# An encoder layer with a gated scan: gate activations spread over the filler, and three pieces of VectorE work handed to GpSimd's DMA and to ScalarE

## The chip, the cores and the metric

The kernel runs on one core of a Trainium2 chip. A core has five engines with queues of their own that run in order and wait for each other by semaphores: TensorE (PE, matmuls; PEld are its weight loads), VectorE (DVE), ScalarE (ACT), GpSimd (POOL) and SyncE (SP, which here only issues DMA transfers). The metric is the device time of one execution in microseconds (us); lower is better.

## The reference

One layer of an encoder over x of 1024 positions by 1024 channels, in float32:

```
h   = rmsnorm(x);  proj = h @ W_in          # 1024 x 8192: glu, q, v, z_f, z_b, og, gA, gB
A   = silu(layernorm(dwconv31(glu(..)))) @ pw
f_d = lb_d + (1 - lb_d) * sigmoid(z_d),  k_d = (1 - lb_d) * sigmoid(-z_d)    # d = forward, backward
S_t = diag(f_t) S_{t-1} + k_t v_t^T,     o_t = S_t^T q_t      # per head, once in each direction
B   = (headnorm(o_fwd + o_bwd) * silu(og)) @ W_o
x   = x + (sigmoid(gA) * A + sigmoid(gB) * B) @ W_out
x   = x + (silu(dwconv3(h2 @ W_gate)) * (h2 @ W_up)) @ W_down,  h2 = rmsnorm(x);  final rmsnorm
```

There are 8 heads of 128 by 128. f is clipped to [1e-6, 1]. What the change touches is the scan, the two lines with f_d and S_t.

## The kernel before, in words

Activations lie transposed: channels on the 128 partitions, positions along the free axis, in halves of 512. Every large matrix product is done as three matmuls of 128x128 by 128x512 (high times high, high times low, low times high, lines 143 to 145), because each operand is split into two parts: ScalarE rounds it (line 121) and VectorE or GpSimd subtracts (line 118). Most of the input projection and the feed-forward product go through a seven-product scheme (`pair_job`) whose weight sums are made by accumulating DMAs that GpSimd issues (line 238).

The stages follow each other: norm and GLU; projection, with the 31-tap convolution on VectorE beside it; then the scan over heads; then output projection and feed-forward.

**The scan.** A head of 1024 positions is two half heads of 512, 16 in all. The scan needs no sequential loop: products of the gates f are formed over blocks of 8 positions, and blocks are then joined pairwise at levels 8, 16, 32 and 64.

- `scan_inputs(i)` (line 741) loads q and the two z (forward, backward) of half head i on SP, and issues on ScalarE, for each direction, sigmoid(-z) into k (line 752), sigmoid(z) (line 753) and f (line 755); then VectorE clamps f (line 762). It is called two half heads ahead.
- `scan_base` (line 765) forms the products over 8 positions in the tile `DE`: a strided copy (line 780), multiplications (`tt`, line 730), a reciprocal (line 786), then `Qh`, `Kh`, `qF` and `kG`. It is stepped along one half head ahead.
- `scan_levels` (line 825) runs the four levels. At each, ScalarE copies kG into `A` (line 835), PE multiplies `A` with `qF` into a PSUM bank (line 838), VectorE multiplies kG and qF up for the next level, and the part of the product that belongs to the level goes into `S_t`: masked copies by VectorE at levels 8, 16 and 32 (lines 865, 869), two copies by ScalarE of 64 partitions at level 64 (line 873). The diagonal of the backward product is kept in `dg` (line 867; one buffer) and added to `S_t` at the end (line 885).
- `scan_states` transposes kG on PE, copies it as `kT` (ScalarE, line 896) and multiplies it with v (line 903); VectorE and ScalarE form the chunk states `Sf` and `Sb`.
- `outputs`, one head later, multiplies `S_t`, `Sf`, `Sb` with v and qF (line 944), squares (line 949, `jk`), takes the power by GpSimd (line 405), scales (line 963) and transposes.

**What sets the order.** PE's order is that of the source (manual schedule): between two steps of the scan, `between(fill)` puts 1.3 pieces of the remaining input projection, the filler `dense`, each of six matmuls, then two steps of the next half head's base, then one step of the previous head's outputs. There are seven such places in a half head. The other engines' orders are set by a planner that starts from the source's order and moves instructions by what it thinks is ready. Each tile has a fixed number of buffers (`zi` 3, `f`, `k` and `q` 2, `S` 3, `DE` and `dg` 1), and the writer of a buffer waits for its last reader.

```
            base = cur.result()
            ahead = Base(ins) if i + 1 < NI else None
            ins = scan_inputs(i + 2) if i + 2 < NI else None
```

Of the kernel before, what the change touches and what calls it, by code (L numbers as in the profile page):

```python
# [44 lines left out]
def tile_hybrid_encoder(  # L45
# [511 lines left out]
    m_32 = cp.tile([P, P], U8, name="m_32")  # L557

    def build_masks():
        it = mp.tile([P, P], I32, tag="tm", name=nm("it"), bufs=4)  # L560
        ip = mp.tile([P, P], I32, tag="tm", name=nm("ip"), bufs=4)
        G.iota(it, pattern=[[1, P]], base=0, channel_multiplier=0)
        G.iota(ip, pattern=[[0, P]], base=0, channel_multiplier=1)
        xo = mp.tile([P, P], I32, tag="tm", name=nm("xo"), bufs=4)
        V.tensor_tensor(xo, it, ip, op=ALU.bitwise_xor)
        fs = mp.tile([P, 4, P], F32, tag="tm", name=nm("fs"), bufs=4)
        V.tensor_copy(fs[:, 0, :], xo)
        V.tensor_tensor(fs[:, 1, :], it, ip, op=ALU.subtract)
        ge = fs[:, 1, :]
# [6 lines left out]
        for m, h in ((m_16, 16.0), (m_32, 32.0)):  # L576
            V.tensor_scalar(fs[:, 2, :], fs[:, 0, :], h, None, op0=ALU.is_ge)
            V.tensor_scalar(fs[:, 3, :], fs[:, 0, :], 2 * h, None, op0=ALU.is_lt)
            V.tensor_tensor(m, fs[:, 2, :], fs[:, 3, :], op=ALU.mult)

    build_masks()

# [155 lines left out]
    def c4(t):  # L738
        return t.rearrange("p (c t) -> p c t", c=4)

    def scan_inputs(i):


        h, half = divmod(i, 2)
        q = page(hp, "q", 2)
        f = hp.tile([P, 2, H], F32, tag="f", name=nm("f"), bufs=2)
        kk = hp.tile([P, 2, H], F32, tag="k", name=nm("k"), bufs=2)
        nc.sync.dma_start(q, d_q[h][half])
        for d in range(2):
            z = page(hp, "zi", 3)  # L750
            nc.sync.dma_start(z, d_z[d][h][half])
            A.activation(kk[:, d, :], z, AF.Sigmoid, scale=-1.0)
            A.activation(z, z, AF.Sigmoid)
            fo = view(f, d * H + 7 * d, [[8, NB], [1 - 2 * d, 8]])
            A.activation(
                fo,
                z.rearrange("p (b e) -> p b e", e=8),
                AF.Identity,
                scale=oml_of(d, h),
                bias=lb_of(d, h),  # L760
            )
        V.tensor_scalar(f, f, MIN_FORGET, 1.0, op0=ALU.max, op1=ALU.min)
        return q, f, kk, kscale[:, h : h + NH + 1 : NH]

    def scan_base(ins):


        q, f, kk, ks = ins
# [11 lines left out]
        V.tensor_copy(ed(2, D + 4), fv(3, 4))  # L780
# [24 lines left out]
        along = [[8, NB], [1, 8]]  # L805
        for d in range(2):
            m0, st = ((0, 1), (7, -1))[d]
            whole = [[8, NB], [st, 8]]
            tt(view(Qh, (1 - d) * H + m0, whole), view(q, m0, whole), view(DE, D + d * H, along))
            yield  # L810
            keys(
                view(Kh, d * H + m0, whole),
                view(kk, d * H + m0, whole),
                ks[:, d : d + 1],
                view(DE, d * H, along),
            )
            yield
        both = [[H, 2], [8, NB], [1, 8]]
        tt(view(qF, 0, both), view(Qh, 0, both), view(fm, 0, [[NB, 2], [1, NB], [0, 8]]))
        yield  # L820
        tt(view(kG, 0, both), view(Kh, 0, both), view(DE, D + 7, [[H, 2], [8, NB], [0, 8]]))
        yield
        yield qF, kG, [(Qh[:, 1 - d, :], Kh[:, d, :]) for d in range(2)], tb

    def scan_levels(base, S_t, Tt):
# [31 lines left out]
        for h in (8, 16, 32, 64):  # L857
# [3 lines left out]
            if h == 8:  # L861
                A.copy(S_t, b)
                for d, m in ((0, m_f), (1, m_b)):
                    bi = inside(d)
                    V.copy_predicated(S_t, over(m), bi)
                    if d == 1:
                        V.copy_predicated(c4(dg), over(m_d), bi)
            elif h < 64:
                V.copy_predicated(S_t, over(m_16 if h == 16 else m_32), b)
            else:  # L870
                for s0 in range(0, P, h):
                    t0 = s0 ^ h
                    A.copy(S_t[s0 : s0 + h, :, t0 : t0 + h], b[s0 : s0 + h, :, t0 : t0 + h])
# [11 lines left out]
        V.tensor_tensor(S_t, S_t, c4(dg), op=ALU.add)  # L885

    def scan_states(i, kG, v, Tt, Sf, Sb):

# [122 lines left out]
            bm[h][half] = split(hx(), hx(), load(d_bm[h][half]), V)  # L1011

    NI = 2 * NH
    cur = Base(scan_inputs(0))
    ins = scan_inputs(1)
    dense.fill(21)
    pending = Stream(iter(()))
    for h in range(NH):
# [4 lines left out]
        for half in range(2):  # L1023
            i = 2 * h + half
            base = cur.result()
            ahead = Base(ins) if i + 1 < NI else None
            ins = scan_inputs(i + 2) if i + 2 < NI else None
# [355 lines left out]
```

## Time and profile before

| | |
|---|---|
| median of 3 runs | 1885.06 us (1883.33 to 1894.11) |
| the profiled execution | 1885.96 us |
| its span in the profile | 1884.2 us |
| PE, DVE, ACT, POOL busy | 95%, 67%, 42%, 11% of the span |
| the scan in the trace | about 560 to 957 us |

The profile is of one execution. A row of a group gives line, engine, operation, what it writes from what, shape and count, then busy time in all, mean ns of one, and the idle time of the engine just before, with what ended it. A row of the waits gives who waited for whom, us in all, times, and the longest. A row of a table of stretches gives, for each engine, busy us and instructions in the stretch, then the granted clock of TensorE, the share of the DMA engines and GB/s. A row of the timeline gives start, length, engine, line and operation; in brackets stands idle time before it and what ended it.

### The profile page before, as it was taken

What the parts mean: (1) busy time and instruction counts of PE and PEld (TensorE: products, weight loads), DVE (VectorE), ACT (ScalarE), POOL (GpSimd) and SP (SyncE); (2) the same over time, 40 slices, a digit from 0 to 9 for tenths busy, and PEclk for the clock granted to TensorE, in tenths of its full rate; (3) what the DMA queues carried; (4) which work ended last, traced back from release to release, by engine and by line L of the source; (5) the groups of instructions that cost most, each with busy time, mean ns of one, the idle gap of its engine ahead of it and who ended that gap; (6) DMA issues with size and microseconds to landing.
All of it is one profiled execution on the core that took longest, in us unless ns stands there. A gap on an engine that the chain in (4) does not pass through costs nothing.

```text
span 1884.2 us, 23705 instructions
## 1 busy us (share of the span) xinstructions
PE 1790.5 (95%) x8543; PEld 1478.6 (78%) x8543; DVE 1270.1 (67%) x1860; ACT 797.2 (42%) x1488; POOL 198.0 (11%) x202
## 2 busy tenths in 40 slices
PE   6988999999999999999989999899999999999996
PEld 4767877877787888888878778688888788788885
DVE  3488999635459999989935556676666767534445
ACT  6333343324554655555442144543443434522124
POOL 3101112213100000000000000111111111000000
PEclk9999999999999999999999999999999999999998
DMA  7747788876572333322228666777676766633134
GB/s 264 222 116 165 181 183 204 188 177 156 176 224 79 118 96 117 109 91 93 84 90 240 194 193 185 165 164 145 145 160 147 154 140 129 216 97 94 55 92 162
DMA packets 322764, 282.99 MB, mean 150 GB/s; under 512 B 14798, under 2 KB 244950, under 8 KB 322646
## 3 DMA queue, kind: packets, MB, share of 16 engines
q1 hardware_dynamic: 270854, 240.57, 41.2%
q0 software_dynamic: 51792, 40.90, 15.6%
q8 instruction: 67, 1.10, 0.2%
q14 instruction: 51, 0.42, 0.1%
HBM read 189.14 MB, written 71.83 MB: 139 GB/s over the span
## 4 chain that ended last, share of the span: by engine, by line
PE 48%; DVE 21%; DMA 18%; ACT 6%; issue 4%; POOL 2%; SPq 0%; ACTq 0%; DVEq 0%; POOLq 0%
PE mm L143 12%; PE mm L144 12%; PE mm L145 12%; DMA wr<-wr 3%; DMA tm<-d_a 3%; DVE wp L118 2%; DMA wr<-sw 2%; PE sc L143 2%; PE sc L145 2%; PE sc L144 2%; DVE kG L730 2%; DMA sw<-in_w_in_dram 2%; DVE acc L645 2%; DMA wr<-in_w_in_dram 2%; DVE qF L730 2%
## 5 line engine op out<-in xcount | busy, mean ns | idle before, releaser
L143 PE MATMUL mm<-hx,wp 128*128 128x512 f32 x1176 | 481.4, 409 | 19.4 <-ACT su L266 5.1
L145 PE MATMUL mm<-hx,wp 128*128 128x512 f32 x1176 | 467.2, 397 | 4.3 <-DVE wp L118 4.3
L144 PE MATMUL mm<-hx,wp 128*128 128x512 f32 x1176 | 466.1, 396 | 2.4 <-POOL hx L118 2.4
L121 ACT CAST wp<-wr 128x1024 fp32r<-128x1024 f32 (+2 forms) x196 | 179.7, 917 | 341.8 <-PE mm L144 207.9
L118 DVE TENSOR_TENSOR wp<-wr,wp 128x1024 fp32r<-128x1024 f32 (+2 forms) x196 | 207.2, 1057 | 118.7 <-ACT wp L121 113.0
L143 PEld LDWEIGHTS mm<-hx,wp 128*128 128x128 f32 x1176 | 225.7, 192 | 69.5 <-ACT su L266 7.2
L145 PEld LDWEIGHTS mm<-hx,wp 128*128 128x128 f32 x1176 | 224.8, 191 | 55.6 <-DVE wp L118 6.7
L144 PEld LDWEIGHTS mm<-hx,wp 128*128 128x128 f32 x1176 | 225.6, 192 | 47.9 <-POOL hx L118 4.7
L645 DVE SCALAR_TENSOR_TENSOR acc<-gl,v_b,acc 128x1024 f32<-128x1024 f32 x120 | 149.3, 1279 | 0.5
L1259 DVE TENSOR_TENSOR xr<-mm,xr 128x512 f32<-128x512 f32 x48 | 33.2, 691 | 80.9 <-PE mm L145 80.9
L238 POOL DMA_DIRECT2D wr<-sw x39 | 34.6, 888 | 491.1 <-DVE wp L118 227.6
L838 PE MATMUL sc<-qF,A 128*128 128x128 f32 x512 | 68.8, 277 | 13.8 <-DVE qF L730 13.2
L838 PEld LDWEIGHTS sc<-qF,A 128*128 128x128 f32 x512 | 64.3, 192 | 21.1 <-issue 17.0
L121 ACT CAST wq<-sw 128x1024 fp32r<-128x1024 f32 x39 | 41.0, 1052 | 78.2 <-PE mm L144 68.5
L835 ACT COPY A<-kG 128x512 f32<-128x512 f32 x64 | 39.6, 618 | 73.3 <-DVE kG L730 50.8
L143 PE MATMUL mm<-hy,wp 128*128 128x512 f32 x156 | 62.3, 399 | 6.7 <-ACT wp L121 5.2
L1181 DVE SCALAR_TENSOR_TENSOR tm<-gp,v_a,tm 128x512 f32<-128x512 f32 x88 | 65.7, 748 | 2.3 <-ACT tm L1177 1.1
L266 ACT COPY su<-mm 128x512 f32<-128x512 f32 x78 | 45.3, 581 | 49.9 <-PE mm L145 49.7
L144 PE MATMUL mm<-hy,wp 128*128 128x512 f32 x156 | 62.1, 398 | 0.0
L145 PE MATMUL mm<-hy,wp 128*128 128x512 f32 x156 | 61.7, 396 | 0.0
L143 PE MATMUL sc<-hy,wq 128*128 128x512 f32 x156 | 61.3, 393 | 0.0
L143 PE MATMUL tr<-hx,wp 128*128 128x512 f32 x156 | 61.3, 393 | 0.0
(289 smaller groups left out, 3587.7 us busy)
## 6 DMA issues: line engine op xcount, KB each, us to landing
wr<-in_w_in_dram SPq DMA_DIRECT2D x55, 512.0 KB, 5.3
sw<-in_ffn_w_up_dram SPq DMA_DIRECT2D x44, 256.0 KB, 3.6
sw<-in_ffn_w_up_dram POOLq DMA_DIRECT2D x22, 512.0 KB, 8.9
wr<-in_ffn_w_up_dram SPq DMA_DIRECT2D x22, 512.0 KB, 5.2
d_g<-ft SPq DMA_DIRECT2D x44, 256.0 KB, 5.6
ev<-d_g SPq DMA_DIRECT2D x44, 256.0 KB, 2.8
wr<-sw POOLq DMA_DIRECT2D x39, 256.0 KB, 3.3
wr<-wr POOLq DMA_DIRECT2D x39, 256.0 KB, 4.4
```

The source lines that it names most:

```text
L118: eng.tensor_tensor(lo, src, hi.bitcast(F32), op=ALU.subtract)
L121: A.copy(hi, src)
L143: T.matmul(acc, whi[:, k, :], ahi, start=first, stop=False, skip_group_check=again)
L144: T.matmul(acc, whi[:, k, :], alo, start=False, stop=False, skip_group_check=again)
L145: T.matmul(acc, wlo[:, k, :], ahi, start=False, stop=last, skip_group_check=again)
L238: G.dma_start(o, a, accum_op=ALU.add)
L266: A.copy(t, acc)
L645: V.scalar_tensor_tensor(acc, g[:, k : k + S], tap(k), acc, op0=ALU.mult, op1=ALU.add)
L730: V.tensor_tensor(o, a, b, op=op)
L835: A.copy(A_t.rearrange("p (b x e) -> p b x e", x=2, e=h), pairs(kG, h))
L838: T.matmul(b[:, c * P : (c + 1) * P].rearrange("p (b x e) -> p b x e", x=2, e=h), A_t[:, c * P : (c + 1) * P], view(qF, c * P, [[2 * h, P ...
L1181: V.scalar_tensor_tensor(c, g[:, o + k : o + k + H], vec("fdw", k * NF + j), c, op0=ALU.mult, op1=ALU.add,)
```

## The change

Four edits in the scan, none elsewhere but for one mask that is no longer built:

1. `scan_inputs` becomes a class `Inputs`. Its three loads are issued at once; its six gate activations come one at a time, one at each of the `between` places, and whatever is left when the base begins. The clamp of f moves to the beginning of `scan_base`.
2. The strided copy into `DE` is done by ScalarE (`A.copy`) in place of VectorE.
3. Level 32 goes into `S_t` by four ScalarE copies of 32 partitions, as level 64 does with two of 64, in place of a masked copy by VectorE; `m_32` is gone.
4. `dg` is added to `S_t` by an accumulating DMA that GpSimd issues, in place of an addition by VectorE.

```diff
-    def scan_inputs(i):
-        h, half = divmod(i, 2)
-        q = page(hp, "q", 2)
-        f = hp.tile([P, 2, H], F32, tag="f", name=nm("f"), bufs=2)
-        kk = hp.tile([P, 2, H], F32, tag="k", name=nm("k"), bufs=2)
-        nc.sync.dma_start(q, d_q[h][half])
-        for d in range(2):
-            z = page(hp, "zi", 3)
-            nc.sync.dma_start(z, d_z[d][h][half])
-            A.activation(kk[:, d, :], z, AF.Sigmoid, scale=-1.0)
-            A.activation(z, z, AF.Sigmoid)
...
+    class Inputs:
+        def __init__(self, i):
+            h, half = divmod(i, 2)
+            q = page(hp, "q", 2)
+            f = hp.tile([P, 2, H], F32, tag="f", name=nm("f"), bufs=2)
+            kk = hp.tile([P, 2, H], F32, tag="k", name=nm("k"), bufs=2)
+            zs = [page(hp, "zi", 3) for _ in range(2)]
+            nc.sync.dma_start(q, d_q[h][half])
+            for d, z in enumerate(zs):
+                nc.sync.dma_start(z, d_z[d][h][half])
+            self.parts = (q, f, kk, kscale[:, h : h + NH + 1 : NH])
+            self.todo = self.make(h, f, kk, zs)
+
+        def make(self, h, f, kk, zs):
+            for d, z in enumerate(zs):
+                A.activation(kk[:, d, :], z, AF.Sigmoid, scale=-1.0)
+                yield
+                A.activation(z, z, AF.Sigmoid)
+                yield
+                fo = view(f, d * H + 7 * d, [[8, NB], [1 - 2 * d, 8]])
+                A.activation(fo, z.rearrange("p (b e) -> p b e", e=8), AF.Identity,
+                    scale=oml_of(d, h), bias=lb_of(d, h))
+                yield
+
+        def step(self):
+            next(self.todo, None)
+
+        def result(self):
+            for _ in self.todo:
+                pass
+            return self.parts
+
+    def scan_base(ins):
+        q, f, kk, ks = ins.result()
         V.tensor_scalar(f, f, MIN_FORGET, 1.0, op0=ALU.max, op1=ALU.min)
-        return q, f, kk, kscale[:, h : h + NH + 1 : NH]
...
-        V.tensor_copy(ed(2, D + 4), fv(3, 4))
+        A.copy(ed(2, D + 4), fv(3, 4))
...
-            elif h < 64:
-                V.copy_predicated(S_t, over(m_16 if h == 16 else m_32), b)
+            elif h == 16:
+                V.copy_predicated(S_t, over(m_16), b)
             else:
                 for s0 in range(0, P, h):
                     t0 = s0 ^ h
                     A.copy(S_t[s0 : s0 + h, :, t0 : t0 + h], b[s0 : s0 + h, :, t0 : t0 + h])
...
-        V.tensor_tensor(S_t, S_t, c4(dg), op=ALU.add)
+        G.dma_start(S_t.rearrange("p c t -> p (c t)"), dg, accum_op=ALU.add)
...
                 pending.fill(1)
+                if ins is not None:
+                    ins.step()
```

More of the change, by code (lines that the diff above doesn't have):

```diff
@@ L556, in tile_hybrid_encoder @@
     m_16 = cp.tile([P, P], U8, name="m_16")
-    m_32 = cp.tile([P, P], U8, name="m_32")
     def build_masks():
@@ L575, in build_masks @@
         V.tensor_tensor(m_b, fs[:, 2, :], fs[:, 3, :], op=ALU.mult)
[L576 to L579, printed above, removed]
+        V.tensor_scalar(fs[:, 2, :], fs[:, 0, :], 16.0, None, op0=ALU.is_ge)
+        V.tensor_scalar(fs[:, 3, :], fs[:, 0, :], 32.0, None, op0=ALU.is_lt)
+        V.tensor_tensor(m_16, fs[:, 2, :], fs[:, 3, :], op=ALU.mult)
     build_masks()
@@ L739, in c4 @@
         return t.rearrange("p (c t) -> p c t", c=4)
-    def scan_inputs(i):
-        h, half = divmod(i, 2)
-        q = page(hp, "q", 2)
-        f = hp.tile([P, 2, H], F32, tag="f", name=nm("f"), bufs=2)
-        kk = hp.tile([P, 2, H], F32, tag="k", name=nm("k"), bufs=2)
-        nc.sync.dma_start(q, d_q[h][half])
-        for d in range(2):
-            z = page(hp, "zi", 3)
-            nc.sync.dma_start(z, d_z[d][h][half])
[L752 to L761, printed above, removed]
+    class Inputs:
[17 more added lines that the diff above has]
+                fo = view(f, d * H + 7 * d, [[8, NB], [1 - 2 * d, 8]])
+                A.activation(
+                    fo,
+                    z.rearrange("p (b e) -> p b e", e=8),
+                    AF.Identity,
+                    scale=oml_of(d, h),
+                    bias=lb_of(d, h),
+                )
+                yield
[5 more added lines that the diff above has]
+            return self.parts
@@ L762, in scan_inputs @@
+    def scan_base(ins):
+        q, f, kk, ks = ins.result()
         V.tensor_scalar(f, f, MIN_FORGET, 1.0, op0=ALU.max, op1=ALU.min)
-        return q, f, kk, kscale[:, h : h + NH + 1 : NH]
-    def scan_base(ins):
-        q, f, kk, ks = ins
         def two(t, *r):
@@ L1013, in tile_hybrid_encoder @@
     NI = 2 * NH
-    cur = Base(scan_inputs(0))
-    ins = scan_inputs(1)
+    cur = Base(Inputs(0))
+    ins = Inputs(1)
     dense.fill(21)
@@ L1026, in tile_hybrid_encoder @@
             ahead = Base(ins) if i + 1 < NI else None
-            ins = scan_inputs(i + 2) if i + 2 < NI else None
+            ins = Inputs(i + 2) if i + 2 < NI else None
             def between(fill):
```

## The prediction

> **What bounds the kernel now.** I read the page first: its head gives the span, its part 1 the busy share of each engine.
>
> ```profile
> span 1884.2 us, 23705 instructions
> PE 1790.5 (95%) x8543; PEld 1478.6 (78%) x8543; DVE 1270.1 (67%) x1860; ACT 797.2 (42%) x1488; POOL 198.0 (11%) x202
> ```
>
> TensorE is busy in 95% of the span, so over the whole kernel nothing but its idle time, some 94 us, can be won without taking matmuls away, and the change takes none. But the change touches one stage alone, the scan over heads, so the second view is the table of stretches, cut where the first and the last matmul of the scan's levels (L838) stand: a stretch ahead of it, the scan, a stretch behind it.
>
> ```profile
> core 0: us, PE busy (x) PEld busy (x) DVE busy (x) ACT busy (x) POOL busy (x), PEclk, DMA share, GB/s
> 530.00:560.00 30.00, 30.00 (x134) 24.75 (x133) 18.94 (x28) 18.77 (x30) 1.07 (x3) 1.00 0.72 227
> 560.00:957.00 397.00, 375.79 (x2403) 330.99 (x2402) 366.39 (x679) 214.88 (x493) 13.73 (x14) 1.00 0.33 101
> 957.00:1000.00 43.00, 38.85 (x200) 32.38 (x199) 15.47 (x26) 19.56 (x49) 1.83 (x2) 0.96 0.39 126
> ```
>
> In the scan two engines are nearly full: PE 375.79 of 397.00, DVE 366.39 of 397.00. ACT has 182 us free and POOL nearly everything. PE's idle time is 397.00 - 375.79 = 21.2 us over 16 half heads; that is the ceiling of any gain here, 1.1% of the kernel. What ends it is in the view of waits, asked for PE in this stretch.
>
> ```profile
> engine line waited for: us in total, times, longest us
> PE sc L838 <- DVE qF L730: 13.2, 11, 2.8
> PE sc L903 <- ACT kT L896: 5.4, 6, 1.3
> PE sc L851 <- ACT Sb L921: 1.8, 2, 1.5
> PE sc L838 <- ACT A L835: 0.5, 1, 0.5
> ```
>
> So two links are late, by about a microsecond at a time: DVE, which must update qF before the next level's matmuls (13.2 us), and ScalarE, which must copy kT before the states' matmuls (5.4 us). The change works on both: it takes load off the first and puts load on the second.
>
> **Part by part.** The groups of DVE in the scan, by line and shape:
>
> ```profile
> L869 DVE COPY_PREDICATED S<-m,sc 128x512 f32<-128x512 uint8 x32 | 23.4, 732 | 0.1
> L885 DVE TENSOR_TENSOR S<-S,dg 128x512 f32<-128x512 f32 x16 | 10.7, 669 | 0.3
> L762 DVE TENSOR_SCALAR f<-f 128x1024 f32<-128x1024 f32 x14 | 9.5, 680 | 4.4 <-ACT f L755 4.4
> L780 DVE COPY DE<-f 128x256 f32<-128x256 f32 x14 | 6.1, 434 | 0.0
> ```
>
> Removed from DVE per half head: one of the two L869 (level 32), L885, L780. Their durations sum to 732 + 669 + 434 = 1835 ns, but neighbours overlap, so what the queue gets back is the distance from one start to the next:
>
> ```profile
> 698.99 0.72 DVE L869 COPY_PREDICATED S<-m,sc 128x512 f32<-128x512 uint8 x1
> 699.60 0.68 DVE L730 TENSOR_TENSOR qF<-qF,tb 128x512 f32<-128x512 f32 x1
> ...
> 702.37 0.70 DVE L885 TENSOR_TENSOR S<-S,dg 128x512 f32<-128x512 f32 x1
> 702.98 1.22 DVE L730 TENSOR_TENSOR qF<-Qh,fm 128x1024 f32<-128x1024 f32 x1
> ```
>
> 0.61 for L869, 0.61 for L885; the same 0.1 off L780 gives about 0.33 (an estimate). That is 1.55 us per half head, 25 us over 16, so DVE goes from 366 to about 341 us busy. L869 stands directly ahead of the qF update that PE waits for. A wait of PE on qF averages 13.2 / 11 = 1.2 us, less than the 1.55 us given back in each half. The longest, 2.8 us, is more than that. I take 10 of the 13.2 us as gone: bounds 0 (if another instruction of that chain is then late) and 13.2.
>
> Added to ScalarE per half head: four copies of 32 partitions by 128 elements from PSUM (level 32), one strided SBUF copy of 256. No row has 32 partitions; the nearest are these.
>
> ```profile
> L835 ACT COPY A<-kG 128x512 f32<-128x512 f32 x64 | 39.6, 618 | 73.3 <-DVE kG L730 50.8 <-PE sc L838 12.7 <-DVE tb L730 9.9
> L873 ACT COPY S<-sc 64x256 f32<-64x256 f32 x32 | 11.6, 363 | 15.6 <-PE sc L838 15.3
> L923 ACT COPY Sb<-sc 128x128 f32<-128x128 f32 x8 | 2.2, 273 | 0.0
> ```
>
> From 128 elements to 256 the cost goes 273 to 363 ns whatever the partitions, so four copies are 4 x 0.27 = 1.1 us; for the strided one I take 0.4 us (between 0.36 and 0.62). So ScalarE gets 1.5 us more per half, 24 us in all: 215 to 239 of under 397. As load that is nothing; what counts is what stands behind it in the queue. Level 32's copies can start once its matmuls end, where DVE's copy did; their bank is not needed before the states' matmuls, behind level 64.
>
> **The moved gates.** In the old order six gate activations stood in one block behind Kh; then came the squares (jk), GpSimd's power (L405) on their sums, four scalings, and only then the second kT copy that PE waits for. One half head of the first kind in each head:
>
> ```profile
> 674.58 1.15 ACT L752 ACTIVATE k<-zi 128x512 f32<-128x512 f32 x2 [1.51 <-DVE Kh L733]
> 675.64 1.14 ACT L753 ACTIVATE zi<-zi 128x512 f32<-128x512 f32 x2
> 677.14 0.82 ACT L755 ACTIVATE f<-zi,lbw 128x512 f32<-128x512 f32 x1
> 678.84 0.37 ACT L873 COPY S<-sc 64x256 f32<-64x256 f32 x1
> 680.35 0.19 ACT L949 ACTIVATION_READ_ACCUMULATOR jk<-tm 128x1 f32 x1
> 682.60 1.28 ACT L963 ACTIVATE tm<-tm,ors 128x128 f32<-128x128 f32 x4 [1.35 <-POOL ors L405]
> 683.78 0.56 ACT L896 COPY kT<-tr 128x512 f32<-128x512 f32 x1
> ```
>
> (The columns are start, length and instruction; `x2` are two in a row.) In the changed program's order the strided copy takes the head of this block and waits for the same Kh; so the old wait is kept, not removed. Of the gates one sigmoid goes behind the squares (-0.5 us), but one or two copies of A for the next half head (0.6 us each in L835) now stand ahead of the last square, with the strided copy (0.4), and in some heads an evacuation stands ahead of the second kT. Against Kh the second kT comes, by these durations, between 0.2 and 2.4 us later than its old 683.78 - 674.58 = 9.2 us. Kh itself comes up to 1.55 us earlier per half given back on DVE. These two cancel within about a microsecond either way, so I take 0 of the 7.2 us of waits on kT and Sb as gone: bounds -7.2 (all gone) and +2.4 x 8 = +19 (no cover from DVE).
>
> The strided copy is also a new wait for DVE, ahead of its second product into DE: behind Kh stands qF, 1.22 us, then kG, against 0.4 us for the copy, so it is ready in time. On SP the loads of q and both z are now issued together, in their old order, ahead of the gates; the first gate waits for Kh today and not for its load:
>
> ```profile
> L752 ACT ACTIVATE k<-zi 128x512 f32<-128x512 f32 x26 | 15.2, 624 | 15.5 <-DVE Kh L733 15.4
> ```
>
> A load that is held up by its buffer for as long as the gates are spread stays hidden, since the buffer's last reader runs in the half head before. I take 0.
>
> The clamp (L762) is later in the source, but DVE's order is the planner's: in the changed program it stands just behind the reciprocal of the head before, a few instructions later than it did. It costs the same 680 ns; its 4.4 us of waiting may come or go with the last gate. DVE has about 2.9 us per half free after the change (397 - 341 over 16, less PE's own gain) to hide that. I take 0. Behind it in DVE's queue stand the Sf updates, which PE reads in the next head.
>
> **The accumulating DMA.** Its like exists already, issued by GpSimd at the same 256 KB, SBUF to SBUF:
>
> ```profile
> L238 POOL DMA_DIRECT2D wr<-sw x39 | 34.6, 888 | 491.1 <-DVE wp L118 227.6
> wr<-sw POOLq DMA_DIRECT2D x39, 256.0 KB, 3.3
> wr<-wr POOLq DMA_DIRECT2D x39, 256.0 KB, 4.4
> ```
>
> 0.9 us of GpSimd and 3.3 to 4.4 us to land. It adds two waits: the matmuls on S (L944), and the next write of dg (one buffer), with the kG update behind it in DVE's queue.
>
> ```profile
> 701.59 0.74 ACT L873 COPY S<-sc 64x256 f32<-64x256 f32 x2 [3.09 <-PE sc L838]
> ...
> 715.14 0.73 DVE L867 COPY_PREDICATED dg<-m_d,ob 128x512 f32<-128x512 uint8 x1
> 718.72 0.38 PE L944 MATMUL ob<-v,S 128*128 128x128 f32 x2
> ```
>
> S is complete at 702.33; 0.9 + 4.4 makes 707.6, 7.5 us ahead of the write at 715.14 and 11 ahead of the first matmul on any S. It stays hidden. In GpSimd's queue the power stands behind this issue, but in the half head shown above S is complete at 679.21 and the last square's sum at 680.54, 1.3 us later, which covers 0.9. Cost 0. Without that cover the power would be late by at most 0.9 us in 8 halves, 7 us. DMA engines are 0.33 busy here and PE waits on no weights.
>
> [...]
>
> ```profile
> L645 DVE SCALAR_TENSOR_TENSOR acc<-gl,v_b,acc x120: 1267/1280/1286, 118.8 to 349.4; 128x1024 f32<-128x1024 f32 x120
> L118 DVE TENSOR_TENSOR wq<-w,wq x39: 683/691/2421, 89.8 to 1592.1; 128x512 fp32r<-128x512 f32 x39
> 461.57 2.42 DVE L118 TENSOR_TENSOR wq<-w,wq 128x512 fp32r<-128x512 f32 x1
> 461.83 3.31 POOL L659 TENSOR_TENSOR tm<-tm,cx 128x512 f32<-128x512 f32 x2
> ```
>
> L645 has two SBUF inputs and runs where GpSimd issues such DMAs all along, yet its slowest is 6 ns above its median: issuing costs DVE nothing. The outlier of 2421 ns stands beside GpSimd's arithmetic (L659). [...]
>
> The three mask instructions removed cost under 1 us once, in a stretch where PE is full: 0.
>
> **Sum.** The profiled execution took 1885.96 us, 1.8 outside its span; the median of the runs is 1885.06, so one stands for the other. 1886 - 10 = **1876 us**, 0.5% faster.
>
> **Rivals.**
> *PE's idle time vanishes.* With DVE 25 us lighter and the gates no block any more, all four rows of waits go: 1886 - 21 = 1865. For it: PE would be the bound by far. Against it: the kT chain still passes through GpSimd's power.
> *ScalarE becomes the late link.* The second kT comes 2.4 us later in every first half of a head: 8 x 2.4 = 19 us, less the 10 of qF: 1895, slower. It decides from where the delay exceeds the 1.55 us that Kh gains. For it: the row with 1.35 us of waiting on POOL; against it: only some heads have the worse order.
> *The change does not do what it says*: the planner puts gates and clamp back, and DVE's free time is only idle, because qF waits on PE's own round trip. 1885.
> *Issuing blocks DVE after all*: 16 x 0.89 = 14 us of the 25 come back, and of the 10 about 4 stay: 1882.
>
> **Chances.** Forecast (1868 to 1882) 0.55; PE's idle time gone (1862 to 1868) 0.15; ScalarE late (1888 to 1905) 0.14; nothing 0.11; blocked issues 0.05. The range leaves out the upper half of the slow case and a little at the bottom: 1864 to 1892. A measurement of this kernel can tell about 1% from no change: below 1866 faster, above 1904 slower. Half of the second case lies below 1866 (0.08); of the slow case a quarter above 1904 (0.04); within, 0.88.
>
> **What would show it.** Right: in the scan DVE is near 341 us and ACT near 239 us busy, the row of PE waiting for qF falls from 13.2 to about 3 us, no DVE wait on the DMA at the dg write, and L903's wait on kT stays near 5 us. Wrong: L903's row grows beyond 15 us, or L838's stays above 10, or a wait of DVE on ScalarE's strided copy appears.

## The result, and the profile after

The changed kernel takes 1886.33 us (median of 20 runs) where the kernel before takes 1882.92 us (20 runs beside them). The ratio of the runs side by side is 1.0022, with a 95% interval of 1.0011 to 1.0032 (that of the two medians is 1.0018). It is 0.2% slower; forecast were 0.5% less. The busy shares on the changed kernel's page:

```profile
PE 1791.3 (95%) x8543; PEld 1481.3 (79%) x8543; DVE 1246.0 (66%) x1809; ACT 823.3 (44%) x1568; POOL 212.5 (11%) x218
```

VectorE lost 24 us and ScalarE took 26. The same stretch as in the prediction, and TensorE's waits in it (columns as there; in the changed file L853 is the levels' matmul, L728 the products, L911 the kT copy, L918 the states' matmul):

```profile
560.00:957.00 397.00, 375.08 (x2392) 331.49 (x2391) 346.83 (x632) 238.93 (x570) 27.85 (x29) 0.99 0.38 110
```

```profile
PE sc L918 <- ACT kT L911: 9.7, 6, 3.0
PE sc L853 <- DVE qF L728: 8.6, 6, 2.8
PE ob L918 <- ACT kT L911: 2.8, 3, 1.7
```

TensorE is idle for 397.00 - 375.08 = 21.9 us, against 21.2 before. The waits on qF fell by 4.6 us, from 13.2 to 8.6, and those on kT rose by 7.1, from 5.4 to 9.7 + 2.8 = 12.5 (two rows: the matmul on the second kT copy of a half head and that on the first). With the smaller rows the listed waits are 20.9 us before and 21.9 after: what came off the one link went to the other.

The parts themselves, by groups of ScalarE's instructions and the list of DMA issues:

```profile
L888 ACT COPY S<-sc 32x128 f32<-32x128 f32 x64 | 16.4, 256 | 17.0 <-PE sc L853 16.2
L795 ACT COPY DE<-f 128x256 f32<-128x256 f32 x16 | 11.2, 700 | 15.1 <-DVE Kh L731 15.0
```

```profile
S<-dg POOLq DMA_DIRECT2D x16, 256.0 KB, 3.5
```

A copy of 32x128 takes 256 ns (the 128x128 row of the prediction had 273), the strided copy 700 ns (and ScalarE waits 15 us in all in front of it), and the accumulating DMA lands 3.5 us after its issue.

**Where kT became late.** One half head of the kernel before and the one that answers to it after, each from the timeline (the squares, the transposes, the scalings that wait for GpSimd's power, the second kT copy; before also the first gate behind Kh and the matmul on kT):

```profile
723.64 0.31 ACT L949 ACTIVATE jk<-tm 128x128 f32<-128x128 f32 x1
...
724.21 1.15 ACT L752 ACTIVATE k<-zi 128x512 f32<-128x512 f32 x2 [0.17 <-DVE Kh L733]
...
730.49 0.30 ACT L949 ACTIVATE jk<-tm 128x128 f32<-128x128 f32 x1
...
731.85 0.60 PE L894 MATMUL tr<-ident,kG 128*128 128x128 f32 x4
...
733.59 1.28 ACT L963 ACTIVATE tm<-tm,ors 128x128 f32<-128x128 f32 x4 [1.29 <-POOL ors L405]
734.78 0.56 ACT L896 COPY kT<-tr 128x512 f32<-128x512 f32 x1
...
735.40 1.16 PE L903 MATMUL sc<-v,kT 128*128 128x128 f32 x8 [0.66 <-ACT kT L896]
```

```profile
723.34 0.68 ACT L795 COPY DE<-f 128x256 f32<-128x256 f32 x1 [1.85 <-DVE Kh L731]
723.92 0.31 ACT L964 ACTIVATE jk<-tm 128x128 f32<-128x128 f32 x1
...
731.40 0.60 PE L909 MATMUL tr<-ident,kG 128*128 128x128 f32 x4
...
733.45 0.31 ACT L964 ACTIVATE jk<-tm 128x128 f32<-128x128 f32 x1
...
735.92 1.28 ACT L978 ACTIVATE tm<-tm,ors 128x128 f32<-128x128 f32 x4 [1.58 <-POOL ors L405]
737.10 0.56 ACT L911 COPY kT<-tr 128x512 f32<-128x512 f32 x1
```

Before, kT is copied 734.78 - 731.85 = 2.93 us after its transposes began; after, 737.10 - 731.40 = 5.70. Both times it stands behind the power. The power is taken of the sums of eight squares, four of each half. Before, the first four were done ahead of Kh (the last of them at 723.64) and the other four by 730.8. After, the strided copy waits 1.85 us for Kh and all eight stand behind it (the first at 723.92, the last at 733.45), mixed with the four copies of level 32.

The same reckoning for all seven half heads that copy kT behind a power, from the timelines, on average: Kh's end lay 5.95 us ahead of the transposes before and 7.35 after, so it came 1.4 us earlier against TensorE (0.5 to 2.3). But the second kT copy began 9.8 us behind Kh's end before and 12.3 after, 2.5 us more (0.4 to 4.2). The difference, 1.1 us, seven times, is 7.6 us, near the 7.1 by which the waits on kT grew. The two long waits, 2.88 and 2.95 us, are in the two half heads with eight squares behind Kh.

**What came on top.** The clock granted to TensorE, in two stretches of 40 us of the changed kernel:

```profile
680.00:720.00 40.00, 37.12 (x230) 32.63 (x229) 33.69 (x66) 22.08 (x47) 2.78 (x3) 0.96 0.41 119
720.00:760.00 40.00, 35.50 (x212) 30.89 (x212) 31.48 (x53) 24.79 (x65) 3.62 (x4) 0.91 0.35 106
```

The other stretches of the scan show 1.00. In the kernel before all show 1.00 but one, with 0.96 and 38.92 us of TensorE (800 to 840 us). The two long waits on kT, 2.88 and 2.95 us, stand in these two stretches. Worked out from the rows, 37.12 x 0.04 + 35.50 x 0.09 = 4.7 us of full speed were lost in them, against 38.92 x 0.04 = 1.6 before. The difference, 3.1 us, is an estimate, and that it comes near the 3.4 us by which the medians differ shows nothing yet: the two traces are of one execution each and their scans differ by 2.0 us, and e4 below has 0.99 over the scan as the changed kernel has, where the kernel before has 1.00, at a time that is not above before (0.9995). No run took the low clock away by itself; how much of the 0.2% it makes stays open.

### The profile page after: what moved, and what is told of

Same layout as the page of the kernel before. It is cut to its first block, busy times and chain, and to the rows that moved or that the text cites. A ratio compares the mean times of both kernels' runs of the same rounds, so it can differ in the third digit from the quotient of the medians.

```text
span 1886.0 us, 23812 instructions
## 1 busy us (share of the span) xinstructions
PE 1791.3 (95%) x8543; PEld 1481.3 (79%) x8543; DVE 1246.0 (66%) x1809; ACT 823.3 (44%) x1568; POOL 212.5 (11%) x218
## 4 chain that ended last, share of the span: by engine, by line
PE 41%; DMA 5%; DVE 3%; ACT 1%; issue 1%; POOL 0%; ACTq 0%; POOLq 0%; DVEq 0%
PE mm L143 10%; PE mm L144 10%; PE mm L145 10%; DMA tm<-d_a 3%; PE sc L143 2%; PE sc L145 2%; PE sc L144 2%; PE tr L144 1%; PE tr L145 1%; PE tr L143 1%; DMA ev<-d_g 1%; PE ob L959 1%; DVE tm L1096 1%; PE sc L853 0%; DMA tm<-d_bm 0%
## 5 line engine op out<-in xcount | busy, mean ns | idle before, releaser
L853 PE MATMUL sc<-qF,A 128*128 128x128 f32 x512 | 68.5, 277 | 9.6 <-DVE qF L728 8.6
L853 PEld LDWEIGHTS sc<-qF,A 128*128 128x128 f32 x512 | 64.4, 192 | 15.6 <-issue 12.5
L1182 DVE TENSOR_TENSOR ft<-su,mm 128x512 f32<-128x512 f32 x22 | 15.1, 687 | 75.8 <-issue 72.3
```

Of the source, the lines that this page charges most:

```text
L853: T.matmul(b[:, c * P : (c + 1) * P].rearrange("p (b x e) -> p b x e", x=2, e=h), A_t[:, c * P : (c + 1) * P], view(qF, c * P, [[2 * h, P ...
```

## The experiments

Waits of TensorE are those of the stretch 560 to 957 us, kT as the sum of its rows. The scan's length runs from its first level matmul to its last. The ratios compare 6 to 12 executions (20 of the changed kernel) with 11 to 35 of the kernel before beside them; waits and lengths are of the one profiled execution. The first level matmul, ahead of which the kernels hardly differ, stands between 552.5 and 562.4 us in these traces, so a few us between two scans, or a single wait, can be chance.

| kernel | ratio to before (95%) | qF, us | kT, us | scan, us |
|---|---|---|---|---|
| before | 1 | 13.2 | 5.4 | 395.8 |
| after | 1.0022 (1.0011 to 1.0032) | 8.6 | 12.5 | 397.8 |
| e1: edit 1 | 1.0019 (1.0004 to 1.0033) | 13.5 | 6.8 | 397.2 |
| e2: edit 2 | 1.0065 (1.0046 to 1.0084) | 8.6 | 7.4 | 405.4 |
| e3: edit 3 | 1.0033 (1.0018 to 1.0049) | 9.0 | 11.8 | 399.1 |
| e4: edit 4 | 0.9995 (0.9983 to 1.0008) | 11.4 | 7.8 | 398.2 |
| e5: edits 1, 3, 4 | 0.9992 (0.9977 to 1.0008) | 9.3 | 9.5 | 390.2 |
| e7: edits 2, 3, 4 | 1.0038 (1.0019 to 1.0056) | 11.8 | 6.5 | 400.0 |
| e8: relief alone | 0.9971 (0.9957 to 0.9986) | 8.6 | 7.8 | 390.3 |
| e9: after, later scalings | 0.9987 (0.9969 to 1.0005) | 5.6 | 8.3 | 390.4 |
| e10: e9, but not in the last head | 0.9983 (0.9967 to 0.9998) | 6.9 | 8.9 | 388.7 |
| e11: e5 and later scalings | 0.9970 (0.9955 to 0.9984) | 7.0 | 7.0 | 388.9 |
| e12: before, later scalings | 0.9995 (0.9979 to 1.0011) | 6.9 | 6.6 | 394.9 |
| e13: e5 and a scratch copy | 1.0006 (0.9993 to 1.0019) | 8.9 | 9.6 | 395.1 |
| e14: no level 16 copy | 0.9992 (0.9977 to 1.0007) | 7.3 | 7.8 | 390.1 |
| e15: no level 32 copy | 1.0014 (1.0001 to 1.0027) | 9.7 | 10.9 | 394.5 |
| e16: no strided copy | 1.0021 (1.0007 to 1.0036) | 10.4 | 9.6 | 396.8 |
| e17: after, no power | 0.9918 (0.9895 to 0.9942) | 9.7 | 2.0 | 387.2 |
| e18: before, no power | 0.9916 (0.9895 to 0.9938) | 11.9 | 0.3 | 384.6 |

**One edit at a time.** The gates one per place, with the later clamp (e1):

```diff
-            ins = scan_inputs(i + 2) if i + 2 < NI else None
+            ins = Inputs(i + 2) if i + 2 < NI else None
...
+                if ins is not None:
+                    ins.step()
```

> The kernel before with the first edit alone: six gate activations one per piece of filler, the clamp at the start of the base; VectorE keeps the strided copy, level 32 and the diagonal. Theory A (the second kT copy stands in ScalarE's queue behind the power and is what came later; gates in one block were not its cause): within 2 us of the kernel before, the row of PE waiting for kT near 5 us. Rival B (the spread gates themselves push kT back): 3 to 6 us slower, that row over 9 us.

The strided copy (e2):

```diff
-        V.tensor_copy(ed(2, D + 4), fv(3, 4))
+        A.copy(ed(2, D + 4), fv(3, 4))
```

> The kernel before with the strided copy alone moved to ScalarE. Theory A: this is the edit that hurts, since the copy waits for Kh at the head of ScalarE's queue with the squares behind it: 3 to 8 us slower, PE waiting for kT over 9 us in the scan. Rival B (gates): within 2 us of the kernel before. Theory D (VectorE's load sets the time): 2 us faster.

Level 32 (e3):

```diff
-            elif h < 64:
-                V.copy_predicated(S_t, over(m_16 if h == 16 else m_32), b)
+            elif h == 16:
+                V.copy_predicated(S_t, over(m_16), b)
```

> The kernel before with level 32 alone copied by ScalarE. Theory A: VectorE gives back 0.6 us ahead of qF, ScalarE gets 1.0 us ahead of the squares: qF waits fall from 13 to about 8 us, kT waits grow from 5 to about 8, time within 2 us of before. Theory D (VectorE's load sets the time): 4 us faster.

The diagonal (e4):

```diff
-        V.tensor_tensor(S_t, S_t, c4(dg), op=ALU.add)
+        G.dma_start(S_t.rearrange("p c t -> p (c t)"), dg, accum_op=ALU.add)
```

> The kernel before with the diagonal alone added by the accumulating DMA. Theory A: nothing on ScalarE changes and VectorE gives back 0.6 us per half head, so 2 to 5 us faster, the wait for qF from 13 to about 8 us. Rival C (the DMA issue stands ahead of the power in GpSimd's queue and delays kT, or its traffic slows others): slower by 3 to 7 us, kT waits over 9 us.

Edit 4 costs nothing and wins nothing that can be measured. Edits 1 to 3 each lose. Theory A has none of the four sizes right: by the ratios e1 loses 3.6 us (at most 2 foreseen; the time is rival B's, the row of kT is not), e2 12 (3 to 8), e3 6 (at most 2), and e4 does not win its 2 to 5. Rival C falls with e4. Edit 2 loses most, and not at kT: a new row appears in TensorE's waits, and the timeline shows its place.

```profile
PE sc L838 <- ACT A L835: 5.7, 7, 1.8
```

```profile
738.53 0.82 ACT L755 ACTIVATE f<-zi,lbw 128x512 f32<-128x512 f32 x1
739.25 0.61 ACT L835 COPY A<-kG 128x512 f32<-128x512 f32 x1
...
739.91 1.16 PE L838 MATMUL sc<-qF,A 128*128 128x128 f32 x8 [1.77 <-ACT A L835]
```

The gates stand directly ahead of the first level's A copy there, for which TensorE waits. The granted clock of e2 over the scan was 0.99 besides, against 1.00 before. What makes the planner put the gates there was not tried. The single losses add up to 1.1%, all four together cost 0.2%.

**Pairs.** Edit 2 undone in the changed kernel (e5), and edit 1 left out (e7):

```diff
-        A.copy(ed(2, D + 4), fv(3, 4))
+        V.tensor_copy(ed(2, D + 4), fv(3, 4))
```

> The changed kernel with edit 2 undone: the strided copy into DE is VectorE's again, edits 1, 3 and 4 stay. Theory A (the strided copy stands in ScalarE's queue waiting for Kh and holds back the squares, the power and the kT copy behind it): the waits of PE on kT fall from 12.5 us to about 7, no wait of ScalarE in front of that copy is left, and the time is below the changed kernel's by 5 to 12 us, at 0.995 to 0.999 of before. Theory D (VectorE's load sets the time): 16 x 0.33 = 5 us more VectorE work makes it slower than the changed kernel, 1.004 or more. If the edits' losses simply add (1.0065 of 1.011 is edit 2's): 0.996.

```diff
-            ins = Inputs(i + 2) if i + 2 < NI else None
+            ins = scan_inputs(i + 2) if i + 2 < NI else None
...
-                if ins is not None:
-                    ins.step()
```

> Edits 2, 3 and 4 without edit 1: the gates stay in one block of six, issued two half heads ahead, as before. If the single losses add, the ratio to before is 1.0065 + 0.0033 - 0.0005 - 1 = 1.009, and edit 1, which alone cost 0.19%, is worth -0.7% once the two copies stand on ScalarE. If edit 1 pushes kT back (theory B), this one is faster than the changed kernel: 1.000 or below, and the waits of PE on kT fall to 5 us. If VectorE's load sets the time (theory D): like the changed kernel, 1.002.

Undoing the copy wins 0.3%, though it puts work back on VectorE: theory D falls. The kT waits stay at 9.5 us, where theory A foresaw about 7, so the copy was not all. With the gates in a block the kernel is, if anything, slower (1.0038, intervals that overlap), and the kT waits are short (6.5): spread gates do push kT back, but the waits on qF (11.8) take the place.

**What the relief alone is worth (e8).** All three pieces leave VectorE and go nowhere:

```diff
+    G.memset(DE, 1.0)
...
-        V.tensor_copy(ed(2, D + 4), fv(3, 4))
...
-            elif h < 64:
-                V.copy_predicated(S_t, over(m_16 if h == 16 else m_32), b)
+            elif h == 16:
+                V.copy_predicated(S_t, over(m_16), b)
+            elif h == 32:
+                pass
...
-        V.tensor_tensor(S_t, S_t, c4(dg), op=ALU.add)
```

> The kernel before with the three pieces of VectorE work left out and put nowhere else: the strided copy into DE (DE is set to 1.0 once instead, so the block products are not the right ones), the masked copy of level 32 into S and the addition of dg to S (both are missing from S). Nothing is added to ScalarE or to a DMA queue, so this shows what the relief alone is worth. My prediction's step (10 of the 13.2 us of waits on qF go): 0.994 to 0.995 and 3 us of qF waits left. Theory D: the same or more, down to 0.989 (all of PE's idle time). If qF waits on PE's own round trip, the DVE relief buys nothing: within 2 us of before, 0.999 to 1.001, and qF waits stay near 10 us.

```profile
PE sc L836 <- DVE qF L729: 8.6, 6, 2.8
PE sc L902 <- ACT kT L895: 7.8, 5, 2.8
```

The waits on qF fall only to 8.6 us, as in the changed kernel, not to 3, and kT's rise although nothing is added to ScalarE. In time 0.29%, some 5.5 us, half of what was forecast for a version that pays nothing. Then single pieces, left out and not replaced (e14 level 16, e15 level 32, e16 the strided copy with DE set to 1.0 once):

```diff
-            elif h < 64:
-                V.copy_predicated(S_t, over(m_16 if h == 16 else m_32), b)
+            elif h == 16:
+                pass
+            elif h == 32:
+                V.copy_predicated(S_t, over(m_32), b)
```

> The kernel before without the masked copy of level 16 into S (that part of S is missing, nothing else changes). Theory E: the late waits of TensorE on qF are those behind level 16, where this copy stands directly ahead of the qF update in VectorE's queue (0.61 us from start to start). Then eight or so of the waits shrink by 0.6 us each: qF waits 13.2 to about 8 us, ratio 0.997 to 0.998. My prediction's reading (a copy ahead of qF at either level, and VectorE's load as such): the same as without level 32's copy.

```diff
-            elif h < 64:
-                V.copy_predicated(S_t, over(m_16 if h == 16 else m_32), b)
+            elif h == 16:
+                V.copy_predicated(S_t, over(m_16), b)
+            elif h == 32:
+                pass
```

> The kernel before without the masked copy of level 32 into S (that part of S is missing, nothing else changes); this is the copy that edit 3 takes from VectorE. Theory E: it stands behind level 16's late qF update, not ahead of it, so nothing is won: 0.9990 to 1.0005, qF waits stay above 11 us. My prediction's reading: 0.61 us per half head off the waits on qF, 0.997 to 0.998.

```diff
+    G.memset(DE, 1.0)
...
-        V.tensor_copy(ed(2, D + 4), fv(3, 4))
```

> The kernel before without the strided copy into DE (DE is set to 1.0 once instead, so the block products are not the right ones); nothing is added to ScalarE. Leaving out all three pieces of VectorE work gave 0.9971. Theory E: the copy starts the base's chain and 0.33 us of it are won in each half head, of which little reaches TensorE: 0.999 to 1.000. If it is the copy that carries the 0.9971 of all three: 0.997 to 0.998, and the waits on qF fall to 9 us.

Without level 16's copy the waits on qF fall most (7.3). Theory E gets the order of the two right but not the sizes: e15 lost 3.5 us of qF waits where it foresaw 2 at most, e14 won no measurable time, and e16 is 0.2% slower where it foresaw 0.1% faster at best. Less work made e15 and e16 slower, by 0.1 and 0.2%, if only just: the intervals begin at 1.0001 and 1.0007. The half head of e15 that answers to the one shown above shows where kT became late:

```profile
722.87 0.63 ACT L752 ACTIVATE k<-zi 128x512 f32<-128x512 f32 x1 [1.75 <-DVE Kh L733]
...
731.02 0.31 ACT L951 ACTIVATE jk<-tm 128x128 f32<-128x128 f32 x1
...
735.24 0.56 ACT L898 COPY kT<-tr 128x512 f32<-128x512 f32 x1
```

```profile
730.57 0.60 PE L896 MATMUL tr<-ident,kG 128*128 128x128 f32 x4
...
735.86 1.16 PE L905 MATMUL sc<-v,kT 128*128 128x128 f32 x8 [2.41 <-ACT kT L898]
```

TensorE is there 1.3 us earlier than before (730.57 for 731.85), and Kh too (its end stands 7.7 us ahead of the transposes, as before). kT is not (735.24 for 734.78), and the wait grows from 0.66 to 2.41. Nothing was added to ScalarE, but the planner gave it another order: a gate, which waits 1.75 us for Kh, stands ahead of seven of the eight squares, where before four were done ahead of it. It is the same in the changed kernel, with the strided copy in the gate's place. In e8, on average over the seven half heads, Kh came 1.5 us earlier against the transposes and kT began 1.8 us later behind Kh.

**The power in front of kT.** First the scalings are only issued later, by two more steps behind the power (e9), then everywhere but in the last head (e10), the same without edit 2 (e11) and in the kernel before (e12):

```diff
         rstd_small(rs, ss, DK)
         yield
         yield
+        if h < NH - 1:
+            yield
+            yield
```

> The changed kernel with the scalings of the outputs two steps later (four yields in place of two behind the power), which puts the kT copies ahead of the scalings that wait for GpSimd's power in ScalarE's queue in five of seven heads, wholly or in part. Theory A, as to the power: the waits of PE on kT fall from 12.5 us to 5 or less, the two stalls of 2.9 us and the low clock behind them go, and the time falls by 7 to 12 us, to 0.996 to 0.998 of before. If the kT copy is late for another reason (the squares or the strided copy ahead of it): kT waits stay above 9 us, ratio 1.001 to 1.003.

> The changed kernel with the scalings of the outputs two steps later in every head but the last (in the run with all heads the scan was 7 us shorter, 390.4 us for 397.8, but TensorE then waited 9.4 us for the split of the last head's outputs at the start of the output projection). Theory A (kT is late because it stands behind the power and the squares): scan near 390 us, the 9.4 us wait gone, ratio to before 0.994 to 0.996. If the shorter scan is given back behind it whatever the last head does: 0.998 to 1.000.

> Edits 1, 3 and 4 (the strided copy is VectorE's), with the scalings two steps later in every head but the last. Edit 2 undone alone gave 0.9992, scan 390.2 us. Theory A: both causes of a late kT copy are gone, waits on kT fall below 5 us, ratio 0.992 to 0.995, below both kernels. If the two remedies remove the same wait: no better than either alone, 0.997 to 0.999.

> The kernel before with the scalings two steps later in every head but the last, none of the four edits. Theory A: only the 5.4 us of waits on kT can go there, and the 13.2 us on qF stay: 0.997 to 0.999. If the edits have no part in what the later scalings win: the same ratio as the changed kernel with later scalings.

In e9 the scan was 7.4 us shorter than in the changed kernel, and behind it stood a new wait, since the last head's outputs now came without filler beside them:

```profile
PE mm L143 <- ACT hx L121: 9.4, 2, 8.7
```

In e10 it is gone, and the scan stays short. The kT waits only fell to 8.9, since the planner still put one or more scalings ahead of kT in most heads. e11 (0.9970) is below both kernels with its whole interval; e10 (0.9983) too. None reaches what theory A foresaw for it, and e11 with 7.0 us on kT is what was foreseen for two remedies of one wait. In the kernel before, the same lines win nothing that can be measured, and against what was expected it is the waits on qF that fall there, to 6.9 us, with no VectorE work taken away (why is said below).

Then a constant in place of the normalising scale, so that the scalings wait for no power (the outputs are not normalised):

```diff
-                    ons[half][:, sl], ons[half][:, sl], AF.Copy, scale=rs[:, half, c : c + 1]
+                    ons[half][:, sl], ons[half][:, sl], AF.Copy, scale=0.5
```

> The changed kernel with a constant in place of the normalising scale of the outputs: the four scalings of a half no longer wait for GpSimd's power (which is still computed and read by nobody), so the outputs are not normalised. At the scan's end this alone takes 2.1 us of waiting off. Theory F (TensorE's gain at qF is only handed on to the kT copy, which cannot come earlier because it stands behind the power): kT waits fall from 12.5 to below 5 us, the scan to 388 us or less, and the time to 0.994 to 0.996 of before. Theory G (the planner's new order of ScalarE, with gates, copies of A and squares ahead of kT, makes it late by itself): kT waits stay above 9 us, ratio 1.000 or more.

> The kernel before with the same constant in place of the normalising scale. Theory F: its kT waits are 5.4 us, so it wins at most these and the 2.1 us at the scan's end: 0.996 to 0.999, and the changed kernel without the power is below it by 3 to 8 us, which is what the four edits are worth once kT is not behind the power. Theory G: it wins as much as the changed kernel does, and the edits still lose about 0.2% against it.

Waits of TensorE, after and before:

```profile
PE sc L853 <- DVE qF L728: 9.7, 9, 2.8
PE sc L918 <- ACT kT L911: 2.0, 2, 1.6
```

```profile
PE sc L838 <- DVE qF L730: 11.9, 10, 2.8
...
PE sc L903 <- ACT kT L896: 0.3, 1, 0.3
```

The waits on kT fall to 2.0 and 0.3 us, and both kernels win 0.8%, more than theory F foresaw for either: kT was late because it stood behind the power, in the kernel before too. Theory G's sign, kT above 9 us in e17, did not come; ScalarE's new order only makes kT's way longer, also without the power (on average kT begins 10.2 us behind Kh in e17 and 8.1 in e18). But theory F also foresaw that the edits would then pay 3 to 8 us, and they pay nothing that can be measured (0.9918 and 0.9916, each within 0.0024), though VectorE is busy for 350.39 us in the one and 371.12 in the other. For 21 us of relief the waits on qF differ by 2.2 us. The timeline shows what holds them, here in the kernels as they were, before and then after:

```profile
738.21 1.06 PE L838 MATMUL sc<-qF,A 128*128 128x128 f32 x8
...
739.97 0.68 DVE L730 TENSOR_TENSOR qF<-qF,tb 128x512 f32<-128x512 f32 x1
...
747.66 0.69 DVE L730 TENSOR_TENSOR qF<-qF,tb 128x512 f32<-128x512 f32 x1
...
748.50 0.68 PE L838 MATMUL sc<-qF,A 128*128 128x128 f32 x4 [1.96 <-DVE qF L730]
```

```profile
743.00 1.20 PE L853 MATMUL sc<-qF,A 128*128 128x128 f32 x8
...
744.24 0.69 DVE L728 TENSOR_TENSOR qF<-qF,tb 128x512 f32<-128x512 f32 x1 [0.24 <-PE sc L853]
...
751.97 0.67 DVE L728 TENSOR_TENSOR qF<-qF,tb 128x512 f32<-128x512 f32 x1
...
752.79 1.13 PE L853 MATMUL sc<-qF,A 128*128 128x128 f32 x8 [1.34 <-DVE qF L728]
```

The first matmul is level 8's, and the qF update of level 8 can start when it ends. From there to the update of level 16, for which the matmul of level 32 waits, VectorE runs with no wait, 7.69 us before and 7.73 after (7.78 and 7.74 in e18 and e17), through the same instructions: products of the next base, the masked copies of level 8, an evacuation, Kh, the masked copy of level 16. None of them is a removed one. Relief elsewhere only lets VectorE be on time at the head of this chain: its update of level 8 came 739.97 - (738.21 + 1.06) = 0.7 us late before and 744.24 - (743.00 + 1.20) = 0.04 after, and the wait behind it went from 1.96 to 1.34. That is all that the relief gave in this place. In e17 and e18 the chain's head is on time in both, and the waits in this place are 1.39 and 1.36.

What does shorten the wait is to take an instruction out of the chain. Without the masked copy of level 16 (e14) it takes 746.15 - 739.06 = 7.09 us, and the wait is 0.73. In e12, where the later scalings move the evacuation out of it, it takes 746.77 - 739.71 = 7.06 us:

```profile
747.60 1.13 PE L838 MATMUL sc<-qF,A 128*128 128x128 f32 x8 [0.66 <-DVE qF L730]
```

Without the copy of level 32 (e15) or the strided copy (e16) the chain stays at 7.72 and 7.64, and the waits at 1.30 and 1.67.

Over the whole scan 11.0 of the 13.2 us before stand at the matmul of level 32, behind such chains, and none of the removed pieces lies in any of them. There 8.6 us stay. The other 2.2 us, 1.9 of them at the matmul of level 64, are gone in the changed kernel; one is the row from which the prediction read that level 32's copy stands ahead:

```profile
700.43 1.13 PE L838 MATMUL sc<-qF,A 128*128 128x128 f32 x8 [1.15 <-DVE qF L730]
```

At level 64 the waits are 1.9 us in e14 too, and 0.6 in e15.

**Duration or place of the strided copy (e13).**

```diff
         V.tensor_copy(ed(2, D + 4), fv(3, 4))
+        A.copy(hp.tile([P, 2, N2], F32, tag="sx", name=nm("sx"), bufs=2), fv(3, 4))
```

> Edits 1, 3 and 4, where VectorE makes the strided copy into DE, and ScalarE makes the same copy a second time into a tile of its own that nobody reads (two buffers), so that it waits for the clamp of f but not for Kh. If edit 2 costs time by the 0.70 us that the copy takes on ScalarE: like the changed kernel, 1.002. If by its place in ScalarE's queue and the wait for Kh (theory A): like edits 1, 3 and 4 without it, 0.9992 within 0.001.

At 1.0006 it lies between the two cases, and its interval reaches both e5's and the changed kernel's. How the 0.3% of edit 2 divides between 700 ns of ScalarE and the wait for Kh stays open.

## Why the prediction was wrong, point by point

- **VectorE and ScalarE busy:** 341 and 239 us foreseen; 346.8 and 238.9 measured. Right for ScalarE, and near for VectorE.
- **"I take 10 of the 13.2 us as gone":** failed. 4.6 went in the changed kernel, 4.6 with no cost elsewhere (e8), 2.2 with kT out of the way (e17 against e18). The working compared the mean wait with what a half head gives back, as if it mattered not where in VectorE's queue the work had stood. It does: "L869 stands directly ahead of the qF update that PE waits for" holds for 1.9 us of waits, at level 64. For 11.0 us the late update is level 16's, behind its own masked copy, at the end of a chain of VectorE work that runs from a matmul of level 8 on (7.7 us in the half head shown); level 32's copy, the diagonal and the strided copy stand outside it. The bound of 0 had named this case, "if another instruction of that chain is then late".
- **"These two cancel, so I take 0" for kT:** failed. The 7.2 us of waits on kT and Sb became 12.5, all on kT. The term for Kh was right, 1.4 us on average for "up to 1.55". The term for kT was too small: 2.5 us on average and up to 4.2, for 0.2 to 2.4. What was left out is that an earlier Kh does not bring the second kT copy forward, since that hangs on the last square and the power, and that in two of the seven half heads the planner would put the first four squares behind the instruction that waits for Kh; the view shown began behind these squares, and the four copies of level 32, counted as load, were not counted ahead of the last square. In the half head shown the strided copy, the four squares and the four copies take 726.46 - 723.34 = 3.1 us (the next instruction starts at 726.46). That the planner does so without any work added to ScalarE (e8, e15) was not foreseen either.
- **Strided copy, 0.4 us:** 0.70 measured, above the upper row. The copy's place in the queue was named in the prediction; what stands behind it was only counted in part.
- **Accumulating DMA at 0, masks at 0, clamp at 0:** right. The DMA lands in 3.5 us, no write of dg waits for it, e4 is 0.9995, and VectorE's waits on f are 3.6 us for 4.4. Issuing did not block VectorE: in e4 it is busy for 353.0 us, 13 less than before.
- **Rivals:** ScalarE as the late link (0.14) is what happened, by its own condition: kT's delay behind Kh exceeds what Kh gains. It is smaller than foreseen, 7 us more of kT waits rather than 19, and only 4.6 of qF came off rather than 10. The rival that nothing happens (0.11) gave nearly the measured time, 1885, and had a part of the reason: 8.6 us of qF waits stay at the end of chains that start from TensorE's own matmul. TensorE's idle time did not vanish. The range held the time, but from the side that was not forecast.
- **The signs for "wrong":** none appeared (kT at 12.5 us, below 15; qF at 8.6, below 10; no wait on the strided copy). They were set too far out to tell. Two of the signs for "right" failed, qF near 3 and kT near 5.

## What to carry to other kernels

Before work is taken off a full engine, follow the late wait back to the last point at which the engine was on time, and count what is removed between the two; relief elsewhere helps only as far as it makes the engine on time at that point. Do this for each late wait by itself: here the same row held waits of two kinds. Then ask of the next late link what it really hangs on: the second kT copy hung on the squares and the power, so that an earlier Kh was no cover for it. Work that fits into an engine's idle time several times over can still come with a loss, if an instruction in its queue waits and others that are due stand behind it: ScalarE had 182 us free in the scan and got 24, its strided copy waited 15.1 us in all for Kh, and the second kT copy began 2.5 us later behind Kh's end. A planner can bring that about by its order alone (1.8 us later in e8, where ScalarE got nothing).

## What the runs showed of the hardware

Low clock came behind waits of TensorE, but not by their length alone. Three matmul groups on kT of one shape, each behind its wait, in the changed kernel, in e13 and in e10:

```profile
737.72 2.08 PE L918 MATMUL sc<-v,kT 128*128 128x128 f32 x8 [2.95 <-ACT kT L911]
```

```profile
737.31 2.08 PE L919 MATMUL sc<-v,kT 128*128 128x128 f32 x8 [2.50 <-ACT kT L912]
```

```profile
733.56 1.16 PE L918 MATMUL sc<-v,kT 128*128 128x128 f32 x8 [2.95 <-ACT kT L911]
```

Behind a wait of 2.50 us the group took 2.08 us for 1.16, at a granted clock of 0.51 (e13, 737 to 739 us); behind one of 2.95 it took 2.08 once, at 0.50 (the changed kernel, 737 to 739), and 1.16 once, at 1.00 (e10, 733 to 735). The clock also fell behind a wait of 1.93 us (the kernel before, whose matmul begins at 800.02), to 0.50 from 802 to 804 us. How long it lasts, in stretches of 2 us of the changed kernel:

```profile
737.00:739.00 2.00, 1.28 (x6) 1.28 (x7) 0.00 (x0) 2.00 (x7) 0.00 (x0) 0.50 0.75 254
739.00:741.00 2.00, 2.00 (x8) 1.71 (x8) 1.53 (x4) 1.97 (x4) 0.00 (x0) 0.50 0.00 0
741.00:743.00 2.00, 2.00 (x8) 1.60 (x7) 0.72 (x2) 0.70 (x2) 0.00 (x0) 0.50 0.47 131
```

The clock is at 0.50 from 737 to 743 us, although TensorE is busy for 5.28 of these 6 us and without a break in the last four. In stretches of 1 us it shows 0.73, six times 0.50, then 0.86 (736 to 744 us), as much as 6.8 us at 0.50; in the kernel before 0.61, 0.50, 0.50 and 0.68 (801 to 805 us), as much as 3.4. Why one wait of 2.95 us was followed by the low clock and another was not, and what ends the drop, no run shows.

Open: in e18 the scan is 11.2 us shorter than before, while TensorE's listed waits within it fell by 7.1 us (20.9 to 13.8). Nearly all of the rest is in TensorE's busy time, 374.82 us before and 371.12 in e18 for 2398 matmuls in each. 1.6 of these 3.7 us are the stretch at 0.96 by the estimate above; what the other 2 are, no view here shows.
